# The gated MLP's up product by seven products of quadrants, its down product in a phase of its own

## The chip, the cores and the metric

The kernel runs on one core of a Trainium2 chip. The core has five engines with queues of their own that work side by side: TensorE (PE) multiplies, VectorE (DVE), ScalarE (ACT) and GpSimd (POOL) work element by element, and SyncE (SP) mostly starts transfers (DMAs). The metric is the device time of one execution in microseconds (us), lower is better. A change of less than 0.2% (about 5 us) cannot be told from none.

## The reference, cut to what matters

One layer on 2048 tokens of 1024 channels: a mixer (attention and pooling heads), a gated MLP, a gated embedding, a last norm. The change is about the MLP; D_FF is 2816, 22 blocks of 128.

```python
h = h + jnp.concatenate([att, pool], axis=-1) @ w_out[i]
hn = _rmsnorm(h, ln_ffn[i])
up = _causal_dwconv(hn @ w_up[i], conv_w[i], conv_b[i])   # w_up: 1024 x 5632, width 3
gate, val = jnp.split(up, 2, axis=-1)
h = h + (jax.nn.silu(gate) * val) @ w_down[i]             # w_down: 2816 x 1024
g = jax.nn.sigmoid(_rmsnorm(h, ln_ple[i]) @ w_ple_gate[i])
```

## The kernel before, in words

All data are float32. A product is made from split operands: each operand is cast on ACT to a form that PE takes whole ("high", line 83), and what the cast left over is found by a subtraction ("low", line 84, on POOL unless another engine is named). Three matmuls (lines 88 to 90: high by high, low by high, high by low) stand for one. Channels lie on the 128 partitions, tokens along the free dimension, in four chunks of 512; a matmul is 128x128 by 128x512.

Everything that the change touches is in `phase_rest`. It starts with the output projection of the mixer (chunk by chunk, eight PSUM banks, sums `xs` to DRAM as h1, sums of squares for the next norm). Then come the MLP's two halves of 1024 tokens. In a half, the normed tokens of two chunks stay in SBUF as 32 split tiles (`hnh`, `hnl`). The 22 blocks f go two by two (`groups`). For each f, `up` computes a gate and a value block: for each of the two, 8 depth tiles by 3 matmuls by 2 chunks into a PSUM tile of two banks. The width-3 convolution then reads PSUM directly: ACT makes the centre tap with the bias (line 1125), DVE adds the two others (lines 1126, 1127) and the two columns that cross the halves (lines 1129 to 1133). Silu (line 1155), the product (line 1156), and the split of the result follow.

`down` multiplies two blocks f at a time by their rows of w_down: 2 chunks by 8 output blocks j, 6 matmuls each into one of four banks, and DVE adds each bank to the tokens' running sum in SBUF (line 1171). It runs one group behind `up`, so the engines prepare one while PE does the other. Weights are loaded in units of 512 KB (w_up twice, once per half; w_down twice as well), two units ahead, in the order of a list `order`. The order of instructions on an engine is made by a scheduler, apart from pieces marked `manual_schedule`, where it is as written. Side work waits in lists (`late`, `between`) that the loops take from, one at a time; `tk.later(n, fn)` puts a piece of work n ticks off.

## Time and profile before

| | |
|---|---|
| time, median of 3 runs | 2613.61 us (2613.14 to 2613.8) |
| profiled execution | 2625.12 us, its span 2623.3 us |
| mean clock granted to PE in it | 0.985 |
| PE busy | 2520.1 us (96%), 12043 matmuls |
| DVE, ACT, POOL busy | 1261.3, 883.3, 711.9 us (48%, 34%, 27%) |
| up products | 3 x 1408 matmuls |
| down products | 3 x 704 matmuls |
| MLP | from about 922 to about 2376 us of the span |

In the profile a row of a group reads: line, engine, operation, output<-inputs, shape, count, then busy time in us and mean duration of one in ns, then the idle time of the engine just before these instructions and what ended it. Matmuls overlap, so their issue interval is read from a window: the window's length over the count. A row of the windows table reads: start:end, its length, then busy time and count for PE, PE's weight loads, DVE, ACT and POOL, then the granted clock, the DMA engines' share and GB/s.

### The profile page before, as it was taken

Reading aid. Unit: us, or ns where it says so; the run is one execution under the profiler, and the core shown is the slowest. Engines: PE = TensorE matmul, PEld = TensorE weight load, DVE = VectorE, ACT = ScalarE, POOL = GpSimd, SP = SyncE. Lnnn points to the kernel's source line nnn. Section 1 sums busy time; section 2 is a strip of 40 time slices with the busy share of each in tenths; the row PEclk is TensorE's granted clock in tenths of the full one; section 3 lists DMA queues with packets and bytes.
Section 4 is the critical chain, followed back from the end, with each engine's and each line's share of the span. In section 5 each row is a group of like instructions: output and inputs, shape, how many; then the busy total and the mean of one; then the engine's idle time right before and its main releaser. Section 6 shows DMA issues by size and latency. Waiting matters only on the chain.

```text
span 2623.3 us, 31408 instructions
## 1 busy us (share of the span) xinstructions
PE 2520.1 (96%) x12043; PEld 2115.6 (81%) x12043; DVE 1261.3 (48%) x2230; ACT 883.3 (34%) x1547; POOL 711.9 (27%) x488
## 2 busy tenths in 40 slices
PE   7999998877889999999999999999999999999998
PEld 7888887766768888888888887888888888878788
DVE  6635438866754433333333335643333333355655
ACT  5423228867812232222222222422222222234332
POOL 3312220244500132222222224432222222242000
PEclk9999999988989999999999999999999999999999
DMA  7534369778464541111111112511111111125332
GB/s 235 172 125 170 135 204 244 160 184 207 140 218 158 193 141 51 49 49 49 49 48 49 49 48 88 187 55 49 49 49 49 49 49 48 49 64 189 121 104 85
DMA packets 164645, 289.30 MB, mean 110 GB/s; under 512 B 33440, under 2 KB 76064, under 8 KB 161424
## 3 DMA queue, kind: packets, MB, share of 16 engines
q1 hardware_dynamic: 127136, 229.98, 28.5%
q10 hardware_dynamic: 18448, 31.57, 3.5%
q0 software_dynamic: 18912, 25.75, 3.1%
q8 instruction: 95, 1.56, 0.3%
q14 instruction: 54, 0.44, 0.1%
HBM read 211.89 MB, written 75.27 MB: 109 GB/s over the span
## 4 chain that ended last, share of the span: by engine, by line
PE 78%; ACT 5%; DMA 4%; DVE 4%; issue 4%; POOL 1%; ACTq 0%; POOLq 0%; DVEq 0%
PE up L88 12%; PE up L89 12%; PE up L90 12%; PE dn L88 5%; PE dn L90 5%; PE dn L89 5%; PE z L90 3%; PE z L88 3%; PE z L89 3%; DMA wb<-wd 2%; PE o L90 2%; PE o L88 2%; PE o L89 2%; PE gp L88 2%; PE gp L90 2%
## 5 line engine op out<-in xcount | busy, mean ns | idle before, releaser
L88 PE MATMUL up<-hnh,hu 128*128 128x512 f32 x1408 | 548.1, 389 | 0.1
L90 PE MATMUL up<-hnh,lu 128*128 128x512 f32 x1408 | 547.8, 389 | 0.0
L89 PE MATMUL up<-hnl,hu 128*128 128x512 f32 x1408 | 547.7, 389 | 0.0
L1126 DVE SCALAR_TENSOR_TENSOR y<-up,vec,y 128x1023 f32<-128x1023 f32 x88 | 112.9, 1283 | 559.1 <-ACT y L1125 559.1
L84 POOL TENSOR_TENSOR lu<-ru,hu 128x1024 fp32r<-128x1024 f32 x88 | 213.4, 2425 | 611.1 <-ACT hu L83 592.6
L1171 DVE TENSOR_TENSOR h<-h,dn 128x512 f32<-128x512 f32 x352 | 235.1, 684 | 258.0 <-PE dn L90 257.2
L88 PEld LDWEIGHTS up<-hnh,hu 128*128 128x128 f32 x1408 | 264.3, 188 | 55.3 <-issue 0.5
L90 PEld LDWEIGHTS up<-hnh,lu 128*128 128x128 f32 x1408 | 264.3, 188 | 55.0
L89 PEld LDWEIGHTS up<-hnl,hu 128*128 128x128 f32 x1408 | 264.3, 188 | 54.7
L88 PE MATMUL dn<-ah,hd 128*128 128x512 f32 x704 | 275.3, 391 | 8.9 <-DVE h L1171 8.8
L89 PE MATMUL dn<-al,hd 128*128 128x512 f32 x704 | 274.0, 389 | 0.0
L90 PE MATMUL dn<-ah,ld 128*128 128x512 f32 x704 | 274.0, 389 | 0.0
L83 ACT CAST hu<-ru 128x1024 fp32r<-128x1024 f32 x88 | 92.5, 1052 | 513.5 <-PE up L89 256.1
L88 PE MATMUL z<-hnh,wh 128*128 128x512 f32 (+1 forms) x480 | 171.0, 356 | 10.2 <-ACT hnh L251 6.1
L89 PE MATMUL z<-hnl,wh 128*128 128x512 f32 (+1 forms) x480 | 170.6, 355 | 2.6 <-DVE hnl L252 2.5
L90 PE MATMUL z<-hnh,wl 128*128 128x512 f32 (+1 forms) x480 | 170.4, 355 | 1.7 <-POOL wl L84 1.7
L88 PEld LDWEIGHTS dn<-ah,hd 128*128 128x128 f32 x704 | 132.1, 188 | 40.7 <-DVE h L1171 13.5
L84 POOL TENSOR_TENSOR al<-y,ah 128x1024 fp32r<-128x1024 f32 x44 | 105.6, 2400 | 180.2 <-ACT ah L83 180.2
L90 PEld LDWEIGHTS dn<-ah,ld 128*128 128x128 f32 x704 | 132.1, 188 | 27.7
L89 PEld LDWEIGHTS dn<-al,hd 128*128 128x128 f32 x704 | 132.1, 188 | 27.1
L84 POOL TENSOR_TENSOR ld<-rd,hd 128x1024 fp32r<-128x1024 f32 x44 | 105.5, 2397 | 160.1 <-ACT hd L83 160.1
L154 DVE TENSOR_TENSOR acc<-acc,sq 128x512 f32<-128x512 f32 (+1 forms) x125 | 91.0, 728 | 50.5 <-ACT sq L153 47.1
(238 smaller groups left out, 4521.2 us busy)
## 6 DMA issues: line engine op xcount, KB each, us to landing
ru<-in_w_up_dram SPq DMA_DIRECT2D x88, 512.0 KB, 3.3
rd<-in_w_down_dram SPq DMA_DIRECT2D x44, 512.0 KB, 3.3
wr<-in_w_in_dram SPq DMA_DIRECT2D x64, 256.0 KB, 4.1
h<-h SPq DMA_DIRECT2D x56, 256.0 KB, 5.0
qhh<-qh SPq DMA_DIRECT2D x16, 512.0 KB, 11.1
qll<-ql SPq DMA_DIRECT2D x16, 512.0 KB, 14.7
v<-vn SPq DMA_DIRECT2D x32, 256.0 KB, 7.9
v<-vf SPq DMA_DIRECT2D x32, 256.0 KB, 8.1
```

The source lines that it names most:

```text
L83: nc.scalar.copy(hi, src)
L84: (low or nc.gpsimd).tensor_tensor(lo, src, fp(hi), op=ALU.subtract)
L88: nc.tensor.matmul(ps, wh, ah, start=first, stop=False)
L89: nc.tensor.matmul(ps, wh, al, start=False, stop=False)
L90: nc.tensor.matmul(ps, wl, ah, start=False, stop=last)
L154: nc.vector.tensor_tensor(acc[:, :n], acc[:, :n], sq[:, :n], op=ALU.add)
L1126: nc.vector.scalar_tensor_tensor(dst[:, 1:], ps[:, : W - 1], cw[1], dst[:, 1:], op0=ALU.mult, op1=ALU.add)
L1171: nc.vector.tensor_tensor(hs[c][j], hs[c][j], ps, op=ALU.add)
```

## The change

The up product of a half and a block f is a product of 2 by 2 quadrants: the tokens in two chunks by the depth in two halves of four tiles (a11, a12, a21, a22), and the depth in two halves by gate and value columns (b11, b12, b21, b22). The change forms it by the Strassen-Winograd scheme: seven products of quadrant sums in place of eight products of quadrants. A "turn" is one f in one half: seven products of 4 depth tiles by 3 matmuls.

- **The tokens' sums** (`prepare`): s1 = a21 + a22, s2 = s1 - a11, s3 = a11 - a21, s4 = a12 - s2 are made by DVE from the normed tokens. For the first half this is done during the output projection's last chunks, four of the seven operands at once split to SBUF, the others stored to DRAM. For the second half it is done in the first turns of the first half, all seven stored to DRAM (28 tiles of 256 KB). `load_operand` and `take_operand` fetch and split them, through six buffers `nt`: three operands in turn 0, seven around turns 21 and 22.
- **The weights' sums** (`sums_t`, `sum_t4`): t1 to t4 are made by POOL from the unsplit weights, then ACT casts and DVE makes the lows (before: POOL). w_up lies in a new layout on the host's side, two tiles of 512 KB for each f, loaded two turns ahead.
- **The products' sums**: the products add into each other in three PSUM banks. a11 b11 is copied out by ACT, then s2 t2 is added on top in the same bank and copied out again, and so with s1 t1 and s4 b22; DVE adds the other banks to the copies in SBUF. Copies and convolution now work on SBUF tiles `ug` and `uv`.
- **The result** of silu and product goes to DRAM (`act`), 22 stores a half.
- **The down product** is a phase of its own behind all 44 turns: chunk by chunk (four), it sums over all 22 f in PSUM, seven banks for the blocks j = 0 to 6 and one ("odd") for j = 7, which runs three f late. `act` and w_down are loaded and split for each chunk (w_down four times, before twice), and DVE adds to h1 once per bank and chunk.
- The order is written by hand for all engines in the up phase. One accumulator for sums of squares is left where there were two, and a scratch space for POOL's transfers is 4096 bytes instead of the default.

The diff, cut to its core (the kernel before's `up` and `down` go, of which the inner loops are shown):

```diff
+                def sums():
+                    emit("a11", k, t["a11"])
+                    emit("a22", k, t["a22"])
+                    s1 = t["s1"] = pool.tile([P, CH], F32, tag="nt", bufs=6, name="nt")
+                    nc.vector.tensor_tensor(s1, t["a21"], t["a22"], op=ALU.add)
+                    emit("s1", k, s1)
+                    nc.vector.tensor_tensor(t["a21"], t["a11"], t["a21"], op=ALU.subtract)
+                    emit("s3", k, t["a21"])
+
+                def rest():
+                    emit("a12", k, t["a12"])
+                    nc.vector.tensor_tensor(t["a11"], t["s1"], t["a11"], op=ALU.subtract)
+                    emit("s2", k, t["a11"])
+                    nc.vector.tensor_tensor(t["a12"], t["a12"], t["a11"], op=ALU.subtract)
+                    emit("s4", k, t["a12"])
+
+                return [load, lambda: norm("a11", "a21"), lambda: norm("a22", "a12"), sums, rest]
...
+        raws, ts, W = {}, {}, {}
+        turns = [(half, f) for half in range(2) for f in range(NF)]
...
+        def sums_t(i):
+
+            if i < len(turns):
+                r0, r1 = raws[i]
+                t13 = fb.tile([P, 1024], F32, tag="t13", name="t13")
+                ts[i] = [t13]
+                eng = nc.gpsimd
+                eng.tensor_tensor(t13[:, :CH], r0[:, CH:], r0[:, :CH], op=ALU.subtract)
+                eng.tensor_tensor(t13[:, CH:], r1[:, :CH], r0[:, CH:], op=ALU.subtract)
+                eng.tensor_tensor(r0[:, CH:], r1[:, :CH], t13[:, :CH], op=ALU.subtract)
...
+                nc.gpsimd.tensor_tensor(t4, r1[:, CH:], r0[:, CH:], op=ALU.subtract)
...
+        def product(pst, p, i, w, first):
+            wh, wl = W.pop((i, w))
+            for k in range(HK):
+                ksl = slice(k * P, (k + 1) * P)
+                ah, al = A[p][k]
+                for n, (x, y) in enumerate(((wh, ah), (wh, al), (wl, ah))):
+                    nc.tensor.matmul(
+                        pst, x[:, ksl], y, start=first and k == 0 and n == 0, stop=k == HK - 1 and n == 2, skip_group_check=True
+                    )
...
+        def take_operand(p):
+            q, fs, got = loads.pop(0)
+            assert p == q
+            operand(p)
+            for k in range(HK):
+                if len(got) <= k:
+                    got.append(fs.pop(0)())
+                split_operand(p, k, got[k])
+                if loads and k:
+                    fetch_ahead(1)
...
+            prev = None
+            for i in range(len(turns) + 1):
+                over = i == len(turns)
+                cur = Shared()
+                if not over:
+                    cur.half, cur.f = turns[i]
+                entering = not over and cur.half == 1 and cur.f == 0
+                if i == 1:
+                    todo.extend([lambda: None] * 6 + prepare(1, fb))
+
+                if not over:
+                    raw_load(i + 2)
+                    cur.a = bank("ua")
+                    product(cur.a, "a11", i, "b11", True)
+                if prev:
+                    nc.scalar.copy(prev.uv[:, lo_], prev.a)
+                    prev.yv = fb.tile([P, 1024], F32, tag="yv", name="yv")
+                    conv_a(prev.yv, prev.uv, NF + prev.f)
+                if not over:
+                    split_w(i + 1, "b11", "t2")
+                if i == 0:
+                    take_operand("a12")
+
+                if prev:
+                    product(prev.c, "a22", i - 1, "t4", False)
+                if not over:
+                    cur.ug = fb.tile([P, 1024], F32, tag="ug", bufs=2, name="ug")
+                    nc.scalar.copy(cur.ug[:, lo_], cur.a)
+                if prev:
+                    conv_b(prev.yv, prev.uv, NF + prev.f, prev.half)
+                if i == 0:
+                    take_operand("s3")
+                if i == NF - 1:
+                    take_operand("a11")
+
+                if not over:
+                    product(cur.a, "s2", i, "t2", False)
+                if prev:
+                    add(prev.ug[:, hi_], prev.c)
+                if entering:
+                    take_operand("a22")
+
+                if not over:
+                    cur.b = bank("ub")
+                    product(cur.b, "a12", i, "b21", True)
+                    nc.scalar.copy(cur.ug[:, hi_], cur.a)
+                if prev:
+                    prev.yg = fb.tile([P, 1024], F32, tag="yg", name="yg")
+                    conv_a(prev.yg, prev.ug, prev.f)
+                if not over:
+                    split_w(i + 1, "t1", "t3")
+                if i == 0:
+                    take_operand("a22")
+                if i == NF - 1:
+                    take_operand("s2")
+
+                if not over:
+                    product(cur.a, "s1", i, "t1", False)
+                    add(cur.ug[:, lo_], cur.b)
+                if prev:
+                    conv_b(prev.yg, prev.ug, prev.f, prev.half)
+                if i == NF - 1:
+                    take_operand("a12")
+
+                if not over:
+                    cur.c = bank("uc")
+                    product(cur.c, "s3", i, "t3", True)
+                    cur.uv = fb.tile([P, 1024], F32, tag="uv", name="uv")
+                    nc.scalar.copy(cur.uv[:, hi_], cur.a)
+                if prev:
+                    nc.scalar.activation(prev.yg, prev.yg, AF.Silu)
+                if i == NF - 1:
+                    take_operand("s1")
+                sums_t(i + 2)
+
+                if not over:
+                    product(cur.a, "s4", i, "b22", False)
+                    add(cur.uv[:, hi_], cur.c)
+                if prev:
+                    nc.vector.tensor_tensor(prev.yg, prev.yg, prev.yv, op=ALU.mult)
+                    nc.sync.dma_start(g.act[prev.f][:, prev.half * 1024 : prev.half * 1024 + 1024], prev.yg)
+                if not over:
+                    split_w(i + 1, "b22", "b21")
+                    split_w(i + 1, "t4")
+                    sum_t4(i + 2)
+                if i == NF - 2:
+                    for p in ("a11", "s2", "a12", "s1", "s3", "s4", "a22"):
+                        load_operand(1, p)
+                    fetch_ahead(6)
+                if i == NF - 1:
+                    take_operand("s3")
+                    take_operand("s4")
+                prev = None if over else cur
...
-                for k in range(KD):
-                    ksl = slice(k * P, (k + 1) * P)
-                    mm3(nc, pss[w][:, c * CH : (c + 1) * CH], wh[:, ksl], wl[:, ksl], *hn2[2 * half + c, k], k == 0, k == KD - 1)
...
+            def term(f, j):
+                js = slice(j * P, (j + 1) * P)
+                w, a = units["d", c, f], acts[c, f]
+                mm3(nc, pds[j], w[0][:, js], w[1][:, js], *a, f == 0, f == NF - 1)
+                if f == NF - 1:
+                    closed(j)
...
+            for f in range(NF + wait):
+                n = c * NF + f
+                if f < NF:
+                    ahead(n + 3)
+                    act_ahead(n + 3)
+                    for j in range(KD - 1):
+                        if f == 0:
+                            pds[j] = psd.tile([P, CH], F32, tag="dn", bufs=KD - 1, name="dn")
+                        term(f, j)
+                if f >= wait:
+                    if f == wait:
+                        pds[KD - 1] = odd("dn7")
+                    term(f - wait, KD - 1)
+                    units.pop(("d", c, f - wait)), acts.pop((c, f - wait))
                 tk.tick()
...
-        def down(fs, acts, hs, half, done=None):
-            wd = [unit("d", half, f) for f in fs]
-            for c in range(2):
-                for j in range(KD):
-                    js = slice(j * P, (j + 1) * P)
-                    ps = bank("dn")
-                    for i in range(len(fs)):
-                        a = [z[:, c * CH : (c + 1) * CH] for z in acts[i]]
-                        mm3(nc, ps, wd[i][0][:, js], wd[i][1][:, js], *a, i == 0, i == len(fs) - 1)
-                    nc.vector.tensor_tensor(hs[c][j], hs[c][j], ps, op=ALU.add)
...
-    nc = bacc.Bacc("TRN2", target_bir_lowering=False, num_devices=1)
+    nc = bacc.Bacc("TRN2", target_bir_lowering=False, num_devices=1, dynamic_dma_scratch_size=4096)
```

ACT's queue in a turn. Before, in the middle of the MLP (hu, hd: weights' highs; y<-up: centre tap; ah: the result's high):

```order
L83 CAST hd_5_10193<-rd_5_10191 128x1024
L1125 ACTIVATE y<-up_6_0_10004,vec 128x1024
L1155 ACTIVATE y<-y 128x1024
L83 CAST hu_8_10258<-ru_8_10256 128x1024
L1125 ACTIVATE y<-up_6_1_10005,vec 128x1024
L83 CAST ah<-y 128x1024
```

And now, one turn of the first half (wu: weights' highs; ua: the bank in which four products are summed; ug, uv: gate and value in SBUF; yg, yv: convolved):

```order
L1322 COPY uv<-ua 128x512
L1247 ACTIVATE yv<-uv,vec 128x1024
L83 CAST wu<-ru 128x1024
L1334 COPY ug<-ua 128x512
L1352 COPY ug<-ua 128x512
L1247 ACTIVATE yg<-ug,vec 128x1024
L83 CAST wu<-t_9567 128x1024
L1375 COPY uv<-ua 128x512
L1377 ACTIVATE yg<-yg 128x1024
L83 CAST wu<-ru_9432 128x1024
L83 CAST wu<-t_9600 128x512
```

The copies out of PSUM are new, and stand in a fixed place between casts and activations.

ACT's queue at the change of halves (s4, a22: operands of the second half, from the buffers nt):

```order
L996 CAST s4h_12353<-nt 128x512
L996 CAST s4h_12355<-nt 128x512
L996 CAST s4h_12357<-nt 128x512
L1322 COPY uv<-ua 128x512
L1247 ACTIVATE yv<-uv,vec 128x1024
L83 CAST wu<-ru 128x1024
L1334 COPY ug<-ua 128x512
L996 CAST a22h_12429<-nt 128x512
L996 CAST a22h_12431<-nt 128x512
```

The casts of the last operands stand ahead of the two copies that turn 22's second product on PE needs.

SP's queue at the end of the last turn (rd: w_down; act: the stored result; ra: the result loaded for the down product):

```order
L1387 DMA act_203<-yg 128x1024
L933 DMA rd_5_15525<-in_w_down_dram 128x1024
L933 DMA rd_6_15564<-in_w_down_dram 128x1024
L1387 DMA act_204<-yg 128x1024
L1430 DMA ra<-act_183 128x512
L1430 DMA ra<-act_184 128x512
L1430 DMA ra<-act_185 128x512
```

The first loads for the down product stand behind the store of the last turn's result.

More of the change, by code (lines that the diff above doesn't have):

```diff
@@ L1082, in phase_rest @@
                     end(grp)
[L1083 removed]
+            out_norm(c, acc)
+        while todo:
+            todo.pop(0)()
+        nctx.close()
         cctx.close()
[L1087 removed]
+        stat[0] = bank2
         fctx = ExitStack()
+        opb = octx.enter_context(tc.tile_pool(name="c_ob", bufs=1, side="right", reuse_waits="tile"))
         fb = fctx.enter_context(tc.tile_pool(name="c_f", bufs=1, reuse_waits="tile"))
[L1090 to L1091 removed]
```

351 lines of the change are left out of this document (207 added, 144 removed).

## The prediction

> **What bounds the kernel now.** I read the page first (busy times, then the chain that ended last), then the windows over the MLP, then PE's waits.
>
> ```profile
> PE 2520.1 (96%) x12043; PEld 2115.6 (81%) x12043; DVE 1261.3 (48%) x2230; ACT 883.3 (34%) x1547; POOL 711.9 (27%) x488
> ...
> PE 78%; ACT 5%; DMA 4%; DVE 4%; issue 4%; POOL 1%; ACTq 0%; POOLq 0%; DVEq 0%
> ...
> 1100.00:1500.00 400.00, 400.00 (x1767) 331.20 (x1766) 140.55 (x180) 89.14 (x84) 117.68 (x50) 1.00 0.15 50
> 1600.00:1640.00 40.00, 35.62 (x151) 27.46 (x150) 30.06 (x38) 10.36 (x15) 20.93 (x14) 1.00 0.38 120
> 1640.00:1700.00 60.00, 58.96 (x264) 48.63 (x263) 37.94 (x45) 25.54 (x35) 26.07 (x14) 1.00 0.55 180
> 2300.00:2340.00 40.00, 38.88 (x171) 31.42 (x170) 19.30 (x24) 11.60 (x13) 16.41 (x8) 1.00 0.15 49
> 2340.00:2380.00 40.00, 37.01 (x165) 29.90 (x164) 33.43 (x47) 18.24 (x27) 15.19 (x10) 1.00 0.48 165
> ...
> PE dn L88 <- DVE h L1171: 8.8, 8, 1.8
> ```
>
> PE is 78% of the chain. In the middle of the MLP it never stops: 400 us hold 1767 matmuls, so one costs 400 / 1767 = 0.2264 us. DVE is busy 35% there, ACT 22%, POOL 29%. PE stands idle only at the ends of the halves: 4.4 + 1.0 + 1.1 + 3.0 = 9.5 us in the four short windows, nearly all down products that wait for a bank that DVE has yet to add. So the MLP's time is a count of matmuls, and each matmul removed is worth its 0.2264 us, as long as the other engines keep up.
>
> **What is removed.** Up is three groups like the first row below; the seven products of a turn are 84 matmuls, in 44 turns 3696.
>
> ```profile
> L88 PE MATMUL up<-hnh,hu 128*128 128x512 f32 x1408 | 548.1, 389 | 0.1
> L1171 DVE TENSOR_TENSOR h<-h,dn 128x512 f32<-128x512 f32 x352 | 235.1, 684 | 258.0 <-PE dn L90 257.2
> ```
>
> 3 x 1408 = 4224 less 3696 are 528 matmuls, 528 x 0.2264 = **119.5 us**. Down keeps its 2112. The 9.5 us of waits at half ends go with the old `down`. DVE's 352 adds become 32, which gives nothing, since these ran beside PE.
>
> **A steady turn** takes PE 84 x 0.2264 = 19.02 us. These rows give the work beside it:
>
> ```profile
> L83 ACT CAST hu<-ru 128x1024 fp32r<-128x1024 f32 x88 | 92.5, 1052 | 513.5 <-PE up L89 256.1 <-PE dn L89 241.2 <-DMA ru<-in_w_up_dram 12.8
> L83 ACT CAST wh<-wr 128x512 fp32r<-128x512 f32 x64 | 38.1, 615 | 40.1 <-DMA wr<-in_w_in_dram 23.3 <-PE z L89 10.1 <-POOL wl L84 2.9
> L387 ACT CAST vt<-z 128x512 fp32r<-128x512 f32 x14 | 8.2, 588 | 49.4 <-PE z L90 41.6 <-DMA vf<-vt 7.4
> L1125 ACT ACTIVATE y<-up,vec 128x1024 f32<-128x1024 f32 x88 | 105.5, 1199 | 3.9 <-PE up L90 3.7
> L1155 ACT ACTIVATE y<-y 128x1024 f32<-128x1024 f32 x44 | 46.7, 1060 | 115.8 <-DVE y L1133 58.5 <-DVE halo L1129 57.3
> L84 DVE TENSOR_TENSOR lwo<-rwo,hwo 128x1024 fp32r<-128x1024 f32 x8 | 9.7, 1220 | 0.4 <-ACT hwo L83 0.3
> L84 DVE TENSOR_TENSOR wl<-wr,wh 128x512 fp32r<-128x512 f32 x20 | 16.0, 817 | 5.2 <-ACT wh L83 4.7
> L1126 DVE SCALAR_TENSOR_TENSOR y<-up,vec,y 128x1023 f32<-128x1023 f32 x88 | 112.9, 1283 | 559.1 <-ACT y L1125 559.1
> L1156 DVE TENSOR_TENSOR y<-y 128x1024 f32<-128x1024 f32 x44 | 54.7, 1243 | 0.6
> L887 POOL TENSOR_TENSOR m<-m,m 128x512 f32<-128x512 f32 x12 | 15.4, 1283 | 0.9
> ```
>
> ACT: 3 casts of 1.05 and one of 0.62, four copies out of PSUM at 0.59 (the row of vt, a read of PSUM of that size), two centre taps of 1.20, silu 1.06: 9.6 us. DVE: lows 3 x 1.22 + 0.82, three adds of 0.68, four taps of 1.28, the product 1.24, some 0.5 for the columns at the edge: 13.4. POOL: four sums of 1.28: 5.1. All are below 19.02. The tightest place is the first copy of `ua` (line 1334). Counted from the turn's start, PE fills the bank until 2.72 us (12 x 0.2264), does the turn before's last product until 5.44, and then adds to the bank. ACT first copies `uv` (0.6 to 1.2, the last sum's end being modelled 0.4 behind its issue), makes a tap (to 2.4) and a cast (to 3.45), and ends the copy at 4.05: 1.3 us in time, with the hand-over. The other two copies are some 1.7 in time, DVE's add before the seventh product 3.7. I take **0** per turn; if this cover is gone, each microsecond late is paid 44 times.
>
> **Start of the up phase, +16 (10 to 20).** Before, up starts with weights already split. Now one of the raw tiles of turn 0 takes memory of the closed output projection, so its load starts at the last matmul.
>
> ```profile
> ru<-in_w_up_dram SPq DMA_DIRECT2D x88, 512.0 KB, 3.3
> nt<-h SPq DMA_DIRECT2D x24, 256.0 KB, 3.0
> ```
>
> Load 3.3, POOL's sums 2 x 1.28, cast 1.05, low 1.22: the first matmul starts at 8 to 9 us. Then the order holds ACT's copy of `ua` behind a cast of turn 1's weights and four casts of a12. That cast waits for POOL's sums of turn 1, and these for turn 0's lows on DVE (one t13 buffer): about 14.5 us. With the four casts of 0.62 and the copy, the second product starts at about 19. Turn 0 has six products, 16.3 us; it ends at 33, 16 late.
>
> **Sums of the second half in turns 1 to 5, +6 (0 to 12).** Each depth tile is 4 norms and 4 sums on DVE:
>
> ```profile
> L160 DVE TENSOR_TENSOR nt<-nt,inv 128x512 f32<-128x512 f32 x24 | 16.0, 689 | 13.0 <-DMA nt<-h 6.7 <-ACT inv L140 6.2
> ```
>
> 8 times about 0.72 are 5.8 us. DVE's 13.4 become 19.2 and, with the spreads of the norm, up to 22 in turns 2 to 4, against 19.02, and it waits in order for loads through six buffers of 3 us a round trip. Low end: it eats the slack alone.
>
> **The change of halves, +15 (8 to 22).** 28 casts of 0.62 raise ACT's 9.6 in turns 21 and 22 (24 of them around 21) to about 24.5, over PE's 19. 28 tiles pass six buffers; each buffer's round is load 3.0, cast 0.6, low 0.7 on DVE or 1.3 on POOL. The last tile of s4 arrives about 35 us into the pair of turns, and behind it in ACT's order stand `uv`'s copy, the centre tap, a cast and the copy that turn 22's second product needs: 39 in place of 24.5.
>
> **End of up to down, +14 (10 to 18).** When the last sum in `ua` is done, PE has one product left (2.7). Behind it runs a serial chain: copy 0.6, tap 1.2, two taps 2.6, add 0.7, tap 1.2, two taps 2.6, silu 1.06, product 1.24, 11.2 in all and 12.7 with 1.5 for seven hand-overs (an estimate). SP's store of that result waits for it, and the first loads for down are queued behind that store, though what they load was stored long before: 3.0 more, cast 0.6, low 0.7. PE starts at 17.0, 14 after its last product.
>
> **Down.** A step f is 24 matmuls, 5.43 us, with a split of weights (1.05 + 1.22) and of the result (0.62 + 0.7): enough. At the three chunk boundaries the norm's column sums wait for the chain of squares and adds, as they did before the gate phase:
>
> ```profile
> 2440.00:2450.00 10.00, 7.34 (x25) 6.01 (x24) 4.79 (x12) 2.64 (x5) 1.01 (x1) 0.66 0.10 28
> ...
> L153 ACT ACTIVATE sq<-h 128x512 f32<-128x512 f32 x49 | 30.5, 630 | 41.5 <-DVE h L1321 27.4 <-DVE acc L154 9.8 <-DVE h L1171 4.0
> L154 DVE TENSOR_TENSOR acc<-acc,sq 128x512 f32<-128x512 f32 x98 | 77.9, 795 | 41.4 <-ACT sq L153 40.1
> ...
> 2442.91 1.86 PE L99 MATMUL st<-ones,acc 128*128 128x1 f32 x8 [2.66 <-DVE acc L154]
> 2444.63 0.77 PE L88 MATMUL gp<-hnh,hg 128*128 128x512 f32 x1
> ...
> 2448.62 0.46 PE L88 MATMUL gp<-hnh,hg 128*128 128x512 f32 x1
> ```
>
> One square buffer makes each of eight blocks a round of 0.63 + 0.80 us, 11.4 in all; the splits of four steps stand between, 1.9 each on DVE: 19. PE's cover is the last step, three late products and two steps, 16: some 3.5 a boundary, 10.5. Before chunk 2 the spread of a norm waits for the odd bank until the last add: 3.5 more. **+14 (4 to 20)**; the first gate product waits for the last add and splits, **+3 (0 to 4)**.
>
> **The clock.** In the last rows, PE is idle for 2.66 us, then does tiny matmuls, and nine intervals from 2444.63 to 2448.62 take 3.99 us in place of 9 x 0.2264 = 2.04. An idle spell of some 3 us costs about 1.9 behind it. The forecast has six (turn 0, half change, end of up, three boundaries): **+11 (4 to 15)**. The Trainium skill, page "TensorE: Matmul & The Clock Gate", section "HAM oscillation — how this bites in real kernels", has it that an idle stretch over some 3.4 us drops the array to half clock, for about as long again. It speaks against this change; an estimate from its figures is 1.7 a spell, 10 in all, and the trace agrees.
>
> The smaller scratch for POOL's transfers I take at 0: no row shows its limit (0 to 11: one landing more on the chain).
>
> ```profile
> wb<-wd POOLq DMA_DIRECT2D x24, 256.0 KB, 11.0
> ```
>
> **The sum.** -119.5 - 9.5 + 16 + 6 + 15 + 14 + 14 + 3 + 11 = -50. The profiled execution took 2625.1, 11.5 over the median of the runs; it would become 2575, and the median **2564 us**. All low ends give -129 + 36 = -93: 2521. All high ends give -129 + 111 + 11 = -7: 2607.
>
> **The rivals.** *Most stalls are covered* (20%): 2521 to 2540. For it speaks that ACT and DVE are less than 40% busy; against it, that in an order written by hand a late instruction holds all behind it. *The transitions cost twice* (13%): start, halves, end of up, boundaries and gate are 62 us; at 1.5 to 2 times these it is 2595 to 2626; it decides where buffers (`nt`, raw) make loads one at a time. Some of this lies within 5 us of 2613.6. *Every turn waits* (11%), the slower side: the copy of `ua` on ACT comes late, because the cast ahead of it waits for POOL's sums of the next turn, or a tap waits for DVE's add. From 50 / 44 = 1.1 us beyond the slack of 1.3 the gain is gone. At 2 us a turn it is 2564 + 88 = 2652. Against it: ACT's row of 1.20 and the cast's 1.05 leave room. *That fewer matmuls aren't issued* is out: the program has 528 fewer.
>
> **How the numbers follow.** The forecast (2540 to 2595) has 56%. Range 2521 to 2606: it leaves out the slow rival, most of the doubled transitions' upper part and a little below. What this kernel's measurement can tell is about 0.2%, 5.2 us: faster 0.84 (56 + 20 + 8 of the 13), same 0.04, slower 0.12.
>
> **What would show it.** Right: 84 matmuls every 19.0 us in a window over turns 10 to 20, 24 every 5.43 us within a down chunk; idle PE of 16, 15 and 14 us at the start, between halves and before down; three waits of `st` for `acc` and slow matmuls behind each. Wrong: a turn above 19.3 us, with PE waiting for ACT's copy (`ug`, `uv`) in each turn; or PE going through the change of halves without a gap.

## The result, and the profile after

The change makes the kernel slower by 0.6%: 2629.24 us (median of 6 runs, 2628.14 to 2635.92) against 2614.07 (6 runs beside them), a ratio of 1.0058 with a 95% interval of 1.0041 to 1.0075. Forecast were 2564 us and a range of 2521 to 2606. The profiled execution took 2628.29 us, its span 2626.5. One run of the eight of a later variant, the column sums one step later, took 4693.47 us; the time given for it below is the median of the other seven.

The page of the changed kernel: busy times, the granted clock and the chain that ended last.

```profile
PE 2432.7 (93%) x11515; PEld 2030.2 (77%) x11515; DVE 1656.6 (63%) x2404; ACT 1098.8 (42%) x1923; POOL 705.3 (27%) x534
...
PEclk9999999988989989999997999999899999999999
...
PE 54%; DVE 14%; issue 11%; ACT 8%; DMA 7%; POOL 2%; SPq 0%; ACTq 0%; POOLq 0%; DVEq 0%
```

The matmuls are gone as forecast: 12043 - 11515 = 528. But PE, which was 78% of the chain, is 54% now, and DVE has risen from 4% to 14%: PE waits. For whom, the waits of PE from the output projection's start into the gate phase say (engine, line, what it waited for: us in total, times, longest):

```profile
PE ua L1236 <- ACT ug L1334: 34.3, 23, 18.6
PE st L99 <- DVE acc L154: 17.2, 5, 6.3
PE dn L88 <- ACT ah L83: 16.9, 1, 16.9
PE ua L1236 <- ACT wu L83: 8.8, 1, 8.8
PE uc L1236 <- DVE uv L1261: 8.6, 3, 3.8
PE ua L1236 <- ACT uv L1375: 4.8, 2, 4.6
...
PE bc L136 <- DVE h L1458: 3.6, 1, 3.6
```

The first row holds one wait of 18.6 us, at the change of halves, and many short ones. Of the 17.2 us of the column sums `st`, two waits of 6.3 and 5.9 lie in down. The windows by stage place them: turn 0, turns 1 to 6, turns 21 and 22, a stretch of 18 turns of the second half, the gap before down, down, and the gate phase.

```profile
934.76:962.95 28.19, 22.56 (x80) 17.44 (x81) 19.97 (x16) 14.08 (x23) 20.61 (x15) 0.78 0.57 179
962.95:1095.51 132.56, 120.64 (x509) 96.89 (x508) 113.54 (x122) 54.53 (x68) 43.13 (x25) 0.97 0.47 159
1362.07:1428.84 66.77, 43.60 (x170) 34.95 (x168) 48.91 (x43) 33.52 (x52) 37.85 (x22) 0.80 0.42 134
...
1466.92:1822.26 355.34, 348.19 (x1514) 282.39 (x1512) 279.69 (x292) 164.68 (x201) 119.67 (x69) 1.00 0.23 79
1843.79:1861.08 17.29, 0.39 (x3) 0.01 (x1) 9.48 (x11) 3.99 (x5) 2.46 (x1) 0.63 0.49 166
1861.08:2370.18 509.10, 492.41 (x2138) 405.88 (x2139) 225.68 (x208) 157.09 (x211) 104.06 (x45) 0.98 0.50 166
...
2370.20:2626.50 256.30, 236.78 (x1261) 203.54 (x1259) 139.70 (x242) 79.72 (x140) 27.43 (x20) 0.97 0.36 118
```

Turns 7 to 20 take 19.04 us each, PE without a gap, as forecast. But the 18 turns of the second half take 355.34 / 18 = 19.74: the wait that I had taken at 0. Turns 1 to 6 hold 132.56 - 6 x 19.04 = 18.3 us too much, turns 21 and 22 66.77 - 38.08 = 28.7.

One such turn of the second half on DVE (start, duration, engine, line, operation), and POOL beside it:

```profile
1619.37 1.94 DVE L1251 SCALAR_TENSOR_TENSOR yg<-ug,vec,yg 128x1023 f32<-128x1023 f32 x1
1621.34 2.20 DVE L1252 SCALAR_TENSOR_TENSOR yg<-ug,vec,yg 128x1022 f32<-128x1022 f32 x1
1623.46 1.24 DVE L1257 SCALAR_TENSOR_TENSOR yg<-halo,vec,yg 128x1 f32<-128x1 f32 x1
...
1631.55 1.27 DVE L1251 SCALAR_TENSOR_TENSOR yv<-uv,vec,yv 128x1023 f32<-128x1023 f32 x1
1632.85 1.28 DVE L1252 SCALAR_TENSOR_TENSOR yv<-uv,vec,yv 128x1022 f32<-128x1022 f32 x1
```

```profile
1618.93 1.29 POOL L1205 TENSOR_TENSOR t<-ru 128x512 f32<-128x512 f32 x1 [8.14 <-DVE wu L84]
1620.19 2.27 POOL L1206 TENSOR_TENSOR t<-ru,ru 128x512 f32<-128x512 f32 x1
1622.54 2.15 POOL L1207 TENSOR_TENSOR ru<-ru,t 128x512 f32<-128x512 f32 x1
```

The same instruction takes 1.27 us for the value and 1.94 and 2.20 for the gate, and a tap of one column takes 1.24 in place of 0.2. The slow ones are those that stand beside POOL's sums of the weights, and these are slow too (2.27 and 2.15 for 1.29). That is what the experiments start from.

In a turn of the first half the same two taps are as slow (1.94 and 2.19 us), and PE has no gap. The difference is what silu on ACT waits for, the second tap there and the last of the two columns here; behind silu stand two casts and the copies that PE needs:

```profile
1207.77 1.06 ACT L1377 ACTIVATE yg<-yg 128x1024 f32<-128x1024 f32 x1 [2.61 <-DVE yg L1252]
...
1605.31 1.06 ACT L1377 ACTIVATE yg<-yg 128x1024 f32<-128x1024 f32 x1 [4.87 <-DVE yg L1258]
```

### The profile page after: what moved, and what is told of

The parts are those of the page before. It is cut to its first block, busy times and chain, and to the rows that moved or that the text cites. A ratio compares the mean times of both kernels' runs of the same rounds, so it can differ in the third digit from the quotient of the medians.

```text
span 2626.5 us, 31943 instructions
## 1 busy us (share of the span) xinstructions
PE 2432.7 (93%) x11515; PEld 2030.2 (77%) x11515; DVE 1656.6 (63%) x2404; ACT 1098.8 (42%) x1923; POOL 705.3 (27%) x534
## 4 chain that ended last, share of the span: by engine, by line
PE 54%; DVE 14%; issue 11%; ACT 8%; DMA 7%; POOL 2%; SPq 0%; ACTq 0%; POOLq 0%; DVEq 0%
PE ua L1236 9%; PE dn L89 5%; PE dn L88 5%; PE dn L90 5%; PE uc L1236 4%; PE z L90 3%; PE z L88 3%; PE z L89 3%; ACT wu L83 3%; PE ub L1236 2%; DMA wb<-wd 2%; PE o L90 2%; DVE yg L1251 2%; DVE yg L1252 2%; PE o L88 2%
## 5 line engine op out<-in xcount | busy, mean ns | idle before, releaser
L83 ACT CAST hd<-rd 128x1024 fp32r<-128x1024 f32 x88 | 92.6, 1052 | 311.6 <-PE dn L89 171.3
L84 DVE TENSOR_TENSOR al<-ra,ah 128x512 fp32r<-128x512 f32 x88 | 124.5, 1418 | 137.4 <-ACT ah L83 137.4
L1205 POOL TENSOR_TENSOR t<-ru 128x512 f32<-128x512 f32 x44 | 59.5, 1352 | 350.8 <-DVE wu L84 335.2
L1236 PE MATMUL ua<-s2h,wu 128*128 128x512 f32 x352 | 121.9, 408 | 34.3 <-ACT ug L1334 34.3
L84 DVE TENSOR_TENSOR wu<-ru,wu 128x1024 fp32r<-128x1024 f32 x88 | 119.8, 1362 | 52.8 <-ACT wu L83 52.8
L84 DVE TENSOR_TENSOR wu<-t,wu 128x1024 fp32r<-128x1024 f32 x88 | 87.2, 991 | 100.8 <-ACT wu L83 58.6
L1236 PE MATMUL uc<-a22h,wu 128*128 128x512 f32 x352 | 118.1, 397 | 8.7 <-DVE uv L1261 8.6
L1236 PE MATMUL ua<-a11h,wu 128*128 128x512 f32 x352 | 117.6, 395 | 9.0 <-ACT wu L83 8.8
L1236 PE MATMUL ua<-s4h,wu 128*128 128x512 f32 x352 | 117.4, 395 | 4.8 <-ACT uv L1375 4.8
L1236 PE MATMUL ub<-a12h,wu 128*128 128x512 f32 x352 | 115.8, 390 | 0.0
```

What stands on the lines that cost most here:

```text
L83: nc.scalar.copy(hi, src)
L84: (low or nc.gpsimd).tensor_tensor(lo, src, fp(hi), op=ALU.subtract)
L1205: eng.tensor_tensor(t13[:, :CH], r0[:, CH:], r0[:, :CH], op=ALU.subtract)
L1236: nc.tensor.matmul(pst, x[:, ksl], y, start=first and k == 0 and n == 0, stop=k == HK - 1 and n == 2, skip_group_check=True)
```

## The experiments

**Theory 1: exclusion.** A DVE instruction with two inputs in SBUF and a POOL instruction hold each other up. Before, the taps and the adds of `down` had one input in PSUM; the change copies the products to SBUF and moves the weights' lows to DVE, so most of DVE's work now has two inputs there, with POOL's sums beside it. **Rivals:** DVE simply has too much to do; the order of the queues, above all ACT's and SP's; the six buffers that the operands are loaded through.

### The weights' sums on DVE

```diff
-                eng = nc.gpsimd
+                eng = nc.vector
...
-                nc.gpsimd.tensor_tensor(t4, r1[:, CH:], r0[:, CH:], op=ALU.subtract)
+                nc.vector.tensor_tensor(t4, r1[:, CH:], r0[:, CH:], op=ALU.subtract)
```

> The four sums of the weights per turn (t1 to t4) go from POOL to DVE; nothing else changes. Theory 1 (a DVE instruction with two inputs in SBUF and a POOL instruction shut each other out): in the changed kernel the two gate taps on DVE take 1.94 and 2.20 us beside POOL's sums, the two value taps 1.27 and 1.28 without them. Without POOL's sums the gate taps fall to 1.28 and the turns of the second half from 19.75 to about 19.05 us, although DVE gets 4 x 0.69 = 2.8 us more work a turn; turns 2 to 6 and the change of halves get a few us shorter; in all 12 to 30 us less than the changed kernel's 2628. Theory 2 (DVE simply has too much in its queue): the turns of the second half grow beyond 19.75, turns 2 to 6 by some 2.8 us each, and the time rises by 10 to 60 us.

Measured: 2610.04 us (2602.42 to 2613.48), 19 less than the changed kernel and 0.9977 [0.9964, 0.999] of the kernel before. A window of the second half as long as the 18 turns above, and the gate's taps in one turn on DVE:

```profile
1442.60:1798.00 355.40, 355.40 (x1570) 294.38 (x1569) 284.91 (x371) 169.84 (x207) 0.10 (x1) 1.00 0.23 80
```

```profile
1619.19 1.28 DVE L1251 SCALAR_TENSOR_TENSOR yg<-ug,vec,yg 128x1023 f32<-128x1023 f32 x1
1620.50 1.28 DVE L1252 SCALAR_TENSOR_TENSOR yg<-ug,vec,yg 128x1022 f32<-128x1022 f32 x1
1621.70 0.21 DVE L1257 SCALAR_TENSOR_TENSOR yg<-halo,vec,yg 128x1 f32<-128x1 f32 x1
```

PE fills the window, 1570 matmuls against 1514 in the same time; the gate taps are back at 1.28. DVE was given 2.8 us of work a turn and these turns became shorter, which excludes the theory of too much work for them. Turns 1 to 6 went from 18.3 to 13.2 us too much, turns 21 and 22 from 28.7 to 23.7: there exclusion is only a part (in turns 21 and 22 POOL still makes half of the lows).

### DVE and POOL by themselves

A kernel of nothing but the sequences that are in dispute (the layer is left out, the output is zeros).

```python
            for n in range(8):
                nc.vector.tensor_tensor(t(f"ss{x}"), src, b, op=ALU.add)      # both in SBUF
            for n in range(8):
                nc.vector.tensor_tensor(t(f"sp{x}"), src, bank, op=ALU.add)   # one in PSUM
...                                                # cp: copy, tap: both in SBUF, tapp: one in PSUM
        for n in range(70):
            nc.gpsimd.tensor_tensor(t("pool2"), pa, pb, op=ALU.add)
        dve("2", go)                               # the same sequences again, beside POOL
```

> Not the layer: only sequences of DVE instructions on 128x512 tiles, eight of each kind (two inputs in SBUF: add ss, tap tap; one in SBUF and one in PSUM: sp, tapp; a copy with one input: cp), first with POOL idle, then with POOL doing 70 additions of 128x512 without a pause; the output is zeros. Theory 1 (exclusion of POOL and of DVE instructions that read two SBUF inputs): alone ss, sp, cp and tap take about 0.69 us; beside POOL ss and tap take 1.3 to 2.4 us (their own time and a POOL instruction's 1.28), sp and tapp stay at 0.69, and POOL's additions get longer beside ss and tap (1.28 to about 2.0) and not beside sp and tapp. Rival (a bandwidth that all share): all DVE kinds get longer by a like share. Rival (it was the place of the gate taps, not POOL): nothing gets longer.

Groups of it: inputs with `a` are the sequences alone, those with `go` the ones beside POOL. The 8 additions of POOL are alone. Its 70 begin with DVE's second time, but 37 of them run after DVE has ended; so the last row takes the 9 that overlap the window of `ss` (47.31 to 60.64 us).

```profile
L1408 DVE TENSOR_TENSOR ss<-a,b 128x512 f32<-128x512 f32 x8 | 5.8, 728 | 0.3
L1408 DVE TENSOR_TENSOR ss<-go,b 128x512 f32<-128x512 f32 x8 | 13.2, 1645 | 13.5 <-POOL go L1427 13.3
L1414 DVE SCALAR_TENSOR_TENSOR tap<-a,b 128x512 f32<-128x512 f32 x8 | 5.5, 692 | 0.2
L1414 DVE SCALAR_TENSOR_TENSOR tap<-go,b 128x512 f32<-128x512 f32 x8 | 13.2, 1647 | 0.2
L1412 DVE COPY cp<-a 128x512 f32<-128x512 f32 x8 | 3.4, 426 | 0.2
L1412 DVE COPY cp<-go 128x512 f32<-128x512 f32 x8 | 10.8, 1347 | 0.2
L1410 DVE TENSOR_TENSOR sp<-a,bank 128x512 f32<-128x512 f32 x8 | 5.5, 686 | 0.2
L1410 DVE TENSOR_TENSOR sp<-go,bank 128x512 f32<-128x512 f32 x8 | 5.5, 686 | 0.2
L1416 DVE SCALAR_TENSOR_TENSOR tapp<-bank,a 128x512 f32<-128x512 f32 x8 | 5.5, 690 | 0.2
L1416 DVE SCALAR_TENSOR_TENSOR tapp<-bank,go 128x512 f32<-128x512 f32 x8 | 5.5, 690 | 0.2
L1425 POOL TENSOR_TENSOR pool<-pa,pb 128x512 f32<-128x512 f32 x8 | 10.1, 1261 | 0.5
...
L1429 POOL TENSOR_TENSOR pool<-pa,pb 128x512 f32<-128x512 f32 x9 | 14.0, 1554 | 0.6
```

With both inputs in SBUF an instruction goes from 0.73 and 0.69 to 1.65 us beside POOL; with one in PSUM it stays at 0.69. A bandwidth shared by all is out. I had not expected that the copy with a single input suffers too (0.43 to 1.35; I had it at 0.69). POOL's additions beside `ss` take 1.55 us, not the 2.0 that I expected: both engines pay, DVE about 0.9 us an instruction and POOL 0.3. The eight adds with POOL beside them span 13.33 us, 1.67 each, less than the 0.73 + 1.26 that one of each takes alone.

The Trainium skill has this rule, page "SBUF — State Buffer", section "Who interferes with whom": DVE's second pair of SBUF ports is POOL's only one, only one of the two can hold it at a time, and a DVE instruction with two SBUF inputs contends for it with a POOL instruction that reads SBUF. The rows agree for `ss`, `tap`, `sp` and `tapp`. Of copies the section says that they too can take the pair, in modes that use both of DVE's ports; 0.43 alone and 1.35 beside POOL fit that.

### ACT's casts ahead of silu

```diff
+                lows = [cast_w(i + 1, "b22", "b21"), cast_w(i + 1, "t4")]
                 if prev:
                     nc.scalar.activation(prev.yg, prev.yg, AF.Silu)
...
-                    split_w(i + 1, "b22", "b21")
-                    split_w(i + 1, "t4")
+                    for low in lows:
+                        low()
```

> On ACT alone, the casts of the next turn's b22, b21 and t4 stand ahead of silu instead of behind it; DVE's order is kept. Theory 1 and the order of the queues both expect it: in the second half silu waits for DVE's last taps of the halo and holds 1.65 us of casts, then the copy that PE waits for; with the casts ahead that copy comes 0.6 us or more earlier, and the turns of the second half fall from 19.75 to 19.05 to 19.2 us, 10 to 14 us in all. If the copy's lateness doesn't come from silu's wait, these turns stay at 19.75.

Measured: 2629.09 us, and the turns of the second half still take 19.76: not the 19.05 to 19.2 expected. ACT in that kernel:

```profile
1605.90 1.06 ACT L1395 ACTIVATE yg<-yg 128x1024 f32<-128x1024 f32 x1 [2.95 <-DVE yg L1273]
1606.86 0.57 ACT L1337 COPY uv<-ua 128x512 f32<-128x512 f32 x1
1608.31 1.25 ACT L1262 ACTIVATE yv<-uv,vec 128x1024 f32<-128x1024 f32 x1 [0.88 <-DVE yg L1404]
1609.46 1.03 ACT L83 CAST wu<-ru 128x1024 fp32r<-128x1024 f32 x1
1610.40 0.57 ACT L1349 COPY ug<-ua 128x512 f32<-128x512 f32 x1
```

With the casts out of the way the tap waits instead for DVE's product of the turn before, the last reader of the one `yv` buffer, and the copy for PE ends at the same place. So the casts ahead of the copy were not what made it late; DVE's chain was.

### The second half's sums spread out

```diff
-                    todo.extend([lambda: None] * 6 + prepare(1, fb))
+                    for s in [lambda: None] * 3 + prepare(1, fb):
+                        todo.extend([s, lambda: None])
```

> The sums of the second half's operands (DVE norms and sums, loads, stores) are taken from the side list at every second product instead of every product, so they lie in turns 1 to 10 instead of 1 to 6. If DVE's work per turn is what makes turns 2 to 6 long (21.5, 22.1, 24.7, 24.5, 20.7 against 19.04: 18.3 us in excess), half of it per turn adds 2.9 us to about 17 and fits: the excess falls to 0 to 6 us, 12 to 18 us gained. The rival, the round trips of loads and stores through six buffers: each step waits as before, wherever it stands, and the excess stays above 12 us.

Measured: 2627.09 us (2620.59 to 2633.37), the turns behind turn 1 at 21.5, 19.0, 21.4, 19.8, 22.1, 21.1, 22.2 and 19.9: 14.7 us too much in place of 18.3. By the limit set before the run (over 12) this speaks for the rival, the round trips through six buffers. But DVE, held up by POOL, has next to no room either: it is busy 15.6 us a turn without these sums, and half of them are 2.9 more in 19.04. The run does not separate the two.

### The column sums one step later

```diff
-            tk.later(2 if c < NCH - 1 else 6, fin)
+            tk.later(3 if c < NCH - 1 else 6, fin)
...
-            if c == 2:
-                renorm(0, 4, dgs)
...
+                if c == 2 and f == 1:
+                    renorm(0, 4, dgs)
                 tk.tick()
```

> In the down phase the norm's column sums are issued one step later (behind the third step of the next chunk, before the odd bank is taken again), and the spread of the norm before chunk 2 behind its second step. If PE only waits there because the squares come too late (6.3, about 5 and 5.9 us, 3.6 at the spread, and half clock behind each), these waits go and 15 to 24 us with them. The rival, that the odd bank or the banks of the next chunk then wait for the same adds: the waits turn up at the next products, and less than 8 us are gained.

Measured: 2616.65 us, 12.6 less, between the 15 to 24 expected and the rival's 8. Down goes from 509.10 to 499.34 us; the waits of `st` fall from 12.2 in two places to 4.2 in three, and 3.5 turn up as waits for lows of the result. A part of the rival is true.

### w_down's lows all on DVE

```diff
-                units[key] = load_w(src, f"{kind}{c}_{i}", nc.vector if nload[0] % 2 else None)
+                units[key] = load_w(src, f"{kind}{c}_{i}", nc.vector)
```

> The changed kernel with all of w_down's lows on DVE in the down phase, instead of every second one on POOL; nothing else. By exclusion, DVE's sums of squares and lows of the result that stand beside a POOL low take 2.46 us instead of 0.68; without POOL they all take 0.68 to 0.69, though DVE gets 1.22 us more in every second step of 5.43. The waits at the chunk boundaries (6.3, 5.9) get 1 to 4 us shorter each, and down falls from 509 to 500 to 506 us. If DVE's load decides, down gets longer than 509.

Measured: 2629.47 us, down 508.61, where 500 to 506 was expected. POOL's 2.4 us lows had stretched single DVE instructions in down to 2.46 us (0.68 alone), but taking them away moves next to nothing: PE still waits 6.2 and 4.4 us for the column sums. In down exclusion is there and isn't what sets the time; the place of the column sums sets a part of it (9.8 us by the run above).

### The scratch space alone, in the kernel before

```diff
-    nc = bacc.Bacc("TRN2", target_bir_lowering=False, num_devices=1)
+    nc = bacc.Bacc("TRN2", target_bir_lowering=False, num_devices=1, dynamic_dma_scratch_size=4096)
```

> The kernel before with only the scratch space for POOL's transfers cut to 4096 bytes, as in the change. In the changed kernel and its variants the output projection ends 924 to 933 us into the span, in the kernel before at 921.7. If the smaller scratch delays POOL's broadcasts in the attention phase, the output projection ends at 924 or later here too and the time rises by 2 to 10 us. If not (the scatter of the attention phase, or the work that the change adds in the output projection), it ends at 920 to 923 and the time stays within 2 us of 2614.

Measured: 2622.98 us (2621.84 to 2625.69) against 2613.41, 1.0037 [1.0022, 1.0051]: 9.6 us by this line alone. Its profiled execution ends the output projection at 920.5, which the expectation took for a sign of no effect; but the kernel before's profiled execution was one of its longest (2625.12 against a median of 2613.61), so the two profiles cannot show it. The runs do. Through what the scratch acts is open, and the combined kernels below keep it small.

### Together

Sums on DVE, w_down's lows on DVE, column sums later, the second half's sums at every third product, turn 0's casts of a12 and of turn 1's weights behind the first copy, and s3, s4 and a22 taken behind the first two copies of turn 22.

```diff
                 if entering:
-                    take_operand("a22")
+                    take_operand("s3")
+                    take_operand("s4")
...
-                if i == 0:
+                if i == 0 or entering:
                     take_operand("a22")
```

> Weights' sums on DVE, and four changes of order: in turn 0 ACT's casts of a12 and of turn 1's weights behind the first copy; the second half's sums at every third product; at the change of halves the operands s3, s4 and a22 taken behind the copies of turn 22; the norm's column sums one step later with the spread behind step 2; w_down's lows all on DVE. Against the run with the sums on DVE alone (median 2610): turn 0 from 26.5 to 18 to 22, the excess of turns 1 to 6 from 13 to 0 to 6, that of turns 21 and 22 from 23.7 to 6 to 14, down from 510 to 490 to 498 us: 2565 to 2580 in all. If exclusion on the chip is only part and loads through the six buffers hold the change of halves, that part keeps over 18 us. If DVE is over its limit with everything on it, turns above 19.3 us turn up beyond turn 2.

Measured: 2575.92 us, 0.9858 [0.9841, 0.9874]. Turn 0 takes 22.3, turns 1 to 6 2.5 us too much, down 493.2; but turns 21 and 22 keep 24.7 + 33.4 - 38.1 = 20.0, over the bound of 18 that I had set for the buffers. The second half's sums now reach past turn 6, and turn 12 takes 19.7; turn 3 (21.0) and turn 23 (20.0) are over 19.3 as well, which the expectation has as a sign that DVE is at its limit in places.

> As comb1, with the lows of the reloaded operands all on DVE instead of half of them on POOL, and the last turn's result stored by ACT's queue instead of SP's. At the change of halves DVE gets 14 x 0.69 = 9.7 us more, and POOL's 14 x 1.28 with their exclusion go: by theory 1 no more than 3 us longer or shorter than comb1 there; by DVE's load alone (52 us of work in two turns of 38) some 8 to 10 us longer. The gap between up and down falls from 17 to about 13, since the first loads for down no longer stand behind a store that waits.

Its two further edits are `nc.vector` for all of `take_operand`'s lows, and the last turn's store by ACT:

```diff
-            (nc.gpsimd if k % 2 else nc.vector).tensor_tensor(lo, t, fp(hi), op=ALU.subtract)
+            nc.vector.tensor_tensor(lo, t, fp(hi), op=ALU.subtract)
...
-                    nc.sync.dma_start(g.act[prev.f][:, prev.half * 1024 : prev.half * 1024 + 1024], prev.yg)
+                    (nc.scalar if over else nc.sync).dma_start(g.act[prev.f][:, prev.half * 1024 : prev.half * 1024 + 1024], prev.yg)
```

Measured: 2566.22 us (2561.87 to 2570.65), 0.9817 [0.98, 0.9835]. Turns 1 to 6, turns 21 and 22, down:

```profile
965.28:1081.99 116.71, 115.55 (x509) 95.28 (x508) 98.59 (x129) 56.84 (x69) 0.00 (x0) 1.00 0.34 111
...
1349.28:1403.98 54.70, 43.43 (x169) 34.53 (x168) 44.23 (x62) 31.49 (x49) 0.00 (x0) 0.91 0.51 163
1818.79:2314.45 495.66, 487.02 (x2138) 401.06 (x2139) 202.50 (x250) 156.99 (x211) 5.03 (x3) 0.99 0.52 171
```

DVE has more work in turns 21 and 22 and they are 3.4 us shorter than in comb1. The gap before down is 12.1 us in place of comb1's 16.2 (17.1 in the changed kernel): the queued store cost 4 us.

### The price of the change of halves

The second half uses the first half's operands, without the reload:

```diff
-                if i == NF - 2:
+                if False:
                     for p in ("a11", "s2", "a12", "s1", "s3", "s4", "a22"):
```

> comb2 without the reload at the change of halves: the second half multiplies the first half's operands again, so 28 loads of 256 KB, their casts and their lows are left out (the result of the second half is then another one). It prices the change of halves by itself: turns 21 and 22 at 19.05 each and the turn behind them too, 16.7 us less than comb2's turns there (21.4 + 33.3 + 19.2), so about 2550. If part of that excess came from something else that lies there (a weight's load, the clock), more than 3 us of it stay.

Measured: 2548.52 us; turns 21 and 22 of this kernel:

```profile
1345.03:1383.11 38.08, 38.08 (x169) 31.53 (x168) 29.59 (x37) 18.09 (x22) 0.00 (x0) 1.00 0.25 83
```

54.70 - 38.08 = 16.6 us: all that was left of the excess there is the reload's.

### Another order at the change of halves

```diff
-                    (nc.scalar if over else nc.sync).dma_start(g.act[prev.f][:, prev.half * 1024 : prev.half * 1024 + 1024], prev.yg)
+                    nc.gpsimd.dma_start(g.act[prev.f][:, prev.half * 1024 : prev.half * 1024 + 1024], prev.yg)
```

with `take_operand` of s1 and s3 behind the first copy of turn 22, s4 and a22 behind the second.

> As comb2, with all stores of the result on POOL's transfer queue instead of SP's, and s1 and s3 taken behind the first copy of turn 22, s4 and a22 behind the second. In comb2 the loads of s4 stand behind a store on SP that waits for DVE (16.4 us), and DVE's lows of s1 hold the add that turn 22's first sum needs (4.8 us). If the order of the queues is what is left of the change of halves, its excess falls from 16.7 to 4 to 9 us and the time to 2554 to 2562. If the round of the six buffers (load, cast, low, next load) holds it, it stays at 12 or more. The gap between up and down stays at 12 to 13. A rival: POOL's transfers are started by POOL itself and could be shut out beside DVE; then stores come late and turns above 19.1 us appear throughout.

Measured: 2563.89 us (2557.37 to 2567.31), 0.9811 [0.9795, 0.9828], not to be told from comb2. Turns 21 to 23:

```profile
1340.65:1412.02 71.37, 61.44 (x253) 48.62 (x252) 60.88 (x85) 41.90 (x61) 1.59 (x3) 0.95 0.45 148
```

71.37 - 57.12 = 14.3 us, where comb2's three turns have 16.7. By the limit that I had set (12 or more) the round of load, cast and low through six buffers holds it. The trace shows how, on DVE and then on ACT:

```profile
1359.48 2.49 DVE L997 TENSOR_TENSOR a12l<-nt,a12h 128x512 fp32r<-128x512 f32 x4
...
1372.33 2.49 DVE L997 TENSOR_TENSOR s1l<-nt,s1h 128x512 fp32r<-128x512 f32 x4
```

```profile
1375.60 0.62 ACT L996 CAST s3h<-nt 128x512 fp32r<-128x512 f32 x1 [4.08 <-DMA nt<-op1s]
...
1379.45 0.58 ACT L1354 COPY ug<-ua 128x512 f32<-128x512 f32 x1
```

A buffer comes free with DVE's low: the next load into it is issued 0.03 to 0.2 us after the low ends. Between these two groups of lows DVE does 10.4 us of the turn's own work, and SP issues no load of an operand from 1362.0 to 1373.0. The next tile of s3 is loaded only then, ACT waits 4.08 us for it, and behind its casts stands the copy that PE waits 5.9 us for. So the round goes through DVE's order, which is written by hand. Neither another order there nor more buffers were tried. No turn behind turn 23 is over 19.05: the stores on POOL's queue make no turn late here.

## Why the prediction was wrong, point by point

Between the profiled executions the terms come out as follows (us; measured from the starts of products, the clock's share within each):

| step of the prediction | forecast | measured |
|---|---|---|
| 528 matmuls fewer | -119.5 | -119.7 |
| what the MLP before held above its matmuls | -9.5 | -18 |
| a steady turn | 0 | +12.6 |
| start of the up phase (wait 8.8, turn 0) | +16 | +20.7 |
| sums of the second half | +6 (0 to 12) | +18.3 |
| change of halves | +15 (8 to 22) | +28.7 |
| up to down | +14 | +17.1 |
| down | +14 (4 to 20) | +30.6 |
| gate phase | +3 (0 to 4) | +9.9 |
| clock, apart | +11 | within the others |
| before the MLP | 0 | +3.6 |
| sum | -50 | +3.8 |

The sum of the measured column is 141.5 - 137.7 = 3.8, the spans differ by 3.2. The median differs by 15.2, mostly because the profiled execution of before was 11.5 us over its median.

**What held.** PE bound the MLP, a matmul was worth 0.2267 us, and no loss was in the count: in turns 7 to 20 the saving is there in full. The places of the waits that the sum names were right, and the gap before down within 3 us; the store ahead of the loads that I named there was worth 4.

**Where it fell, first: "I take 0 per turn".** I priced DVE's and POOL's work apart, each from rows in which the other was mostly idle or DVE had an input in PSUM, and added neither to the other. Beside POOL's sums the gate taps cost 4.14 us in place of 2.56. In the first half the turn's slack takes that up; in the second, where silu also waits for the two columns from the first half (1.24 for one of them in place of 0.21), it doesn't, and each of 18 turns is 0.7 long, 12.6 in all. The rival that I set up for this (a late copy of `ua`) had the place right, the wait row names it, and 11% and 2 us a turn as price; its cause, and that it would come in the second half alone, was not in it. The run with the sums on DVE shows the cause.

**Second: "8 times about 0.72 are 5.8 us".** DVE's 13.4 was 15.6 beside POOL (217.72 us busy in the 14 turns 7 to 20), so the sums had no slack to go in: 18.3 us, above the high end of 12. The runs split it: without POOL's sums 13.2 are left, spread over every second product alone 14.7, both together, with every third product, 3.2 (turn 12 included). Each cure alone does little; I had bounded this term as though DVE's load and POOL's hold on it could not meet. What part the round trips through the buffers have is not shown.

**Third: the change of halves.** The mechanism was right (28 tiles through six buffers, the fourth tile of s4 late, the copy behind it), its size was not: 28.7 against 15, high end 22. The fourth tile of s4 was cast 47.0 us into the pair of turns; the forecast has it arrive at about 35, a figure for which it gives no working. Exclusion makes 5.0 of it, with the sums off POOL; the order of the takes about 3.7 more; lows off POOL 3.4. These are differences of single traces; three kernels that differ from the changed one elsewhere show 26.2 to 28.4 here, so each part is uncertain by some 2 us. 16.6 are the reload's, which the run without it prices.

**Fourth: down and the gate phase.** Down's 30.6 misleads, as the rows of the table count differently. PE's waits in down are 12.2 us for the column sums (6.3 and 5.9, where "some 3.5 a boundary" stood for three), 3.6 for the spread and 0.9 for lows: 16.7, where 14 was forecast. Another 5.9 are 26 small matmuls for norms (26 x 0.2267), which the count of 2112 leaves out; the MLP before has 38 of them, 8.6 us, in its row of 18. The rest, some 8 us, are mostly matmuls at the lower clock behind the waits, which the forecast has under "clock". The later column sums take away 9.8 us. I had first thought exclusion to be the cause here as well; the run with the lows on DVE says it isn't. The gate phase's 9.9, where 3 was forecast, goes with waits of PE for lows and casts of late weights (1.7, 1.5, 1.2 and 1.2 us), which the forecast did not name and the kernel before doesn't have; no run tests it.

**Fifth: the scratch.** Taken at 0 with a high end of 11; 9.6 in the runs. That the bound was there didn't help, as I summed with 0. It is no row of the table, since the profile of the kernel before (span 2623.3 us) is no shorter than that with the small scratch (2621.2).

**The range.** The high end had all high ends added up (2607), so it fell because single ones were too low: steady turns had none, and the sums (18.3 over 12), the change of halves (28.7 over 22) and the gate phase (9.9 over 4) passed theirs. The first three share DVE beside POOL, for which no term had a price, and so went wrong together.

The mean granted clock fell from 0.985 to 0.968; in turns 21 and 22 it was 0.80, in turn 0 0.78. Behind the wait before down seven intervals in a row are 0.43 us in place of 0.2267: that a wait is followed by slow matmuls was forecast rightly.

## What to carry to other kernels

Before adding up per-engine loads, list which DVE instructions will have both inputs in SBUF and what POOL does at that moment: side by side they cost more on both engines, above all on DVE. Copying a product out of PSUM early frees a bank, but turns every later pass over it into such an instruction; the weights' sums, which look free on an idle POOL, were cheaper on the busy DVE here. A scheme that saves matmuls in a loop pays at each entry, exit and change of operands. Adding up the high ends of these prices protects only if each was set with the neighbours' work running, and not from rows in which they were idle.

With POOL kept out and the order mended, the same scheme takes 2564 to 2566 us, 1.8 to 1.9% less than the kernel before. That this is also the forecast's 2564 us is chance: it took several more changes to the kernel, none of which the forecast contains.

## What the runs showed of the hardware

- DVE beside a POOL that adds without a pause: 0.73 to 1.65 us (add, two SBUF inputs), 0.69 to 1.65 (tap), 0.43 to 1.35 (copy), no change with an input in PSUM. In the changed kernel even a tap of one column took 1.24 and up to 2.30 us in place of 0.21.
- POOL pays less: its additions beside DVE's adds take 1.55 us in place of 1.26. An add of each together takes 1.67 us, less than one after the other.
- A smaller scratch for POOL's transfers cost 9.6 us (interval 1.0022 to 1.0051) in a kernel that was otherwise unchanged.
